# RWKV chunk maps taken off the state chain, early transfers placed elsewhere, and output transposes for two chunks

## The chip, the cores and the metric

One NeuronCore of a Trainium2 chip runs the whole program. Its engines are TensorE (PE, with its weight loads listed as PEld), VectorE (DVE), ScalarE (ACT), GpSimd (POOL) and SyncE (SP, which here only issues transfers); 16 DMA engines move data. The metric is the device time of one execution in microseconds, the median of several runs. PE's granted clock is given as a share of its full 2.4 GHz; 0.5 is its other level, 1.2 GHz.

## The reference

One layer of an encoder is computed for 1024 prompt rows and 64 sample rows of width 1024. All branches take columns of one projection.

```python
u = rms_norm(h);  z = u @ w_in
A: RWKV-7 (8 heads of 64): per step
   sa = S @ -kk;  S = S*w + sa*(kk*a) + v*k;  y = S @ r      # S: 64 x 64 state
   y = group_norm(y)*lnx_w + lnx_b + (sum(r*k*r_k))*v
B: forgetting attention, softmax(q.k/8 + c[t] - c[s]), causal
C: indexer scores -> top 256 keys -> grouped-query attention + T5 bias
h = h + concat(A*silu(gA), B*silu(gB), C*silu(gC)) @ w_out;  out = rms_norm(h)
```

The new states (RWKV state, keys, values, log forget gates, index keys) are outputs too.

## The kernel before

**Stages.** (1) Rows are loaded, normed and transposed; the indexer projects its keys and queries, and `weave` alternates its scoring with "fill". (2) RWKV: 17 units of four 64-step chunks (a unit is one pair of heads and four chunks; the last unit is the sample, one chunk for each pair). (3) Forgetting attention ("fox"). (4) Sparse attention ("dsa") and the output product.

**Fill** is the projection of all other columns, written as generators whose every step is one eighth of a projection: three matmuls at L154. `pump(rate)` adds to a credit after each step of a main generator and takes fill steps for it; `need(name)` drains fill up to a name. Fill is PE's work for moments in which the stage itself has none.

**RWKV.** In iteration u `braid` interleaves the steps of `tail` (unit u-2), `chain` (u-1), `chunk_invert` and `value_rows` (u) and `prepare` (u+1) by evenly spread positions, and the top-k search beside them; every step pumps R_A/10 = 0.7 fill steps. `chunk_invert` inverts a 64x64 triangular matrix per chunk and head by five doubling levels in float16 and gives `UD`. `chain` carries the state S: for each chunk a product of S with `QR` (`pa`, L1545), VectorE's `za` (L1546), a product with `UD` (`pb`, L1550), two VectorE copies to `UV` (L1555), products with `BA` into the state (L1558) and VectorE's new S (L1563), then the outputs from `BA` and `QR` (L1567, L1569). All five products work on 64x64 or 128x64 pieces of PE's array, one for each head; a float32 product is two instructions. `tail` norms the outputs, transposes one chunk at a time (four transposes of 128x64) and applies scale and bias on ScalarE (L1617).

**First transfers.** The index keys `KI` and `KIL` are computed on partitions 0 to 63 and copied to 64 to 127 by two transfers from GpSimd's queue (L443, L444). `relative_bias` multiplies a small table and stores it 128 times over (L1244, 1536 KB) to DRAM for the dsa stage. SP issues nearly all other transfers, in one order. The index keys' output is stored at L457, L458. `rwkv_pools` opens RWKV's buffers, loads `wabr` and splits it (L1262, L1264).

The instructions are put in order at build time by a list scheduler: an instruction that is written later can be placed earlier on its engine if its inputs are ready there.

Of the kernel before, what the change touches and what calls it, by code (L numbers as in the profile page):

```python
# [12 lines left out]
F32 = mybir.dt.float32  # L13
# [11 lines left out]
P = 128  # L25
# [60 lines left out]
class K:  # L86
# [149 lines left out]
    def braid(self, work, rate, side=None):  # L236


        order = sorted(((k + 0.5) / n * (0.4 if work[j][0] == "rows" else 1), j) for j, (_, _, n) in enumerate(work) for k in range(n))
# [30 lines left out]
    def setup(self):  # L270
# [12 lines left out]
        self.lnx = cp.tile([64, 16], F32, name="lnx")  # L283
# [4 lines left out]
        with ExitStack() as c2:  # L288
# [17 lines left out]
            lrows = xb[:16, 2 * P:2 * P + 64]  # L306
            nc.sync.dma_start(out=lrows[0:8, :], in_=I["a_lnx_w"].rearrange("x (a p) -> (x a) p", p=64))
            nc.sync.dma_start(out=lrows[8:16, :], in_=I["a_lnx_b"].rearrange("x (a p) -> (x a) p", p=64))
            ps = self.pt.tile([P, 4, P], F32, tag="xps", name="ps_setup").rearrange("p a b -> p (a b)")
            nc.tensor.transpose(ps[:, :46], rows[:46, :], self.ident[:46, :46])  # L310
            nc.tensor.transpose(ps[:64, 64:80], lrows, self.ident[:16, :16])
            nc.vector.tensor_copy(self.par[:, :46], ps[:, :46])
            nc.vector.tensor_scalar(self.lnx, ps[:64, 64:80], 0.5, None, op0=OP.mult)
# [84 lines left out]
    def indexer(self):  # L398
# [6 lines left out]
        with ExitStack() as c2:  # L405
# [10 lines left out]

            def keys(t0, n):
                ps = yield from self.proj(wm, t0, n)
                nc.scalar.copy(mT[:76, t0:t0 + n], ps[:76, :n])
                self.split2(ps[0:64, :n], None, KI[0:64, t0:t0 + n], KIL[0:64, t0:t0 + n])  # L420
# [19 lines left out]
            nc.scalar.copy(KI[0:64, 1088:1600], ps[:64, :])  # L440
            nc.vector.tensor_tensor(KIL[0:64, 1088:1600], ps[:64, :], KI[0:64, 1088:1600], op=OP.subtract)
# [15 lines left out]
            nc.sync.dma_start(out=O["p_c_kidx"][0, 0].rearrange("(a p) d -> p a d", p=P), in_=mrow[:, 0:8, 0:64])  # L457
            nc.sync.dma_start(out=O["s_c_kidx"][0, 0], in_=mrow[:64, 8, 0:64])  # L458
            for i in list(range(2, 8)) + ["s"]:
                if i == 4:  # L460
                    self.forget(ip, mrow)
                if i == 5:
                    self.relative_bias()
# [22 lines left out]
    def forget(self, ip, mrow):  # L486
# [26 lines left out]
        v.scalar_tensor_tensor(x, a, -2.0, x, op0=OP.mult, op1=OP.add)  # L513
        nc.sync.dma_start(out=O["p_b_logf"][0, 0].rearrange("(a p) h -> p a h", p=P), in_=x[:, 0:8, :])
# [714 lines left out]
    def relative_bias(self):  # L1229

        nc = self.nc
        self.d_t5 = self.dram.tile([P, 8, 384], F32, tag="d_t5", name="d_t5")
        with ExitStack() as c2:
            p = self.pool("t5", ctx=c2, right=True)
            pp = self.pool("t5p", space=PSUM, ctx=c2, right=True)
            tb = p.tile([32, 8], F32, name="t5tab")
            oh = p.tile([32, 384], F32, name="t5oh")
            nc.sync.dma_start(out=tb, in_=self.I["t5_table"])
            nc.sync.dma_start(out=oh, in_=self.I["onehot"])
            ps = pp.tile([P, 512], F32, name="t5ps")  # L1240
            nc.tensor.matmul(ps[:8, :384], tb, oh, start=True, stop=True)
            vv = p.tile([8, 384], F32, name="t5v")
            nc.vector.tensor_copy(vv, ps[:8, :384])
            nc.sync.dma_start(out=self.d_t5.rearrange("q h r -> h q r"), in_=vv.rearrange("h (o r) -> h o r", o=1).broadcast_to([8, P, 384]))  # L1244


    def rwkv_pools(self, c2):
# [20 lines left out]
        for t in self.ND:  # L1268
            nc.gpsimd.memset(t, 0.0)
# [12 lines left out]
    def elem(self, one, slots, x):  # L1282
# [13 lines left out]
        zt = one.tile([P, 2, N], F32, tag="zt", name="zt", bufs=2)  # L1296
        QR = one.tile([P, 4, 3, 64], F32, tag="QR", name="QR", bufs=3)
# [75 lines left out]
    def chunk_rows(self, one, x):  # L1373
# [9 lines left out]
        BA = one.tile([P, 2, 4, 128], F32, tag="BA", name="BA", bufs=3)  # L1383
# [29 lines left out]
    def value_rows(self, one, x, sample):  # L1413
# [13 lines left out]
        P1 = one.tile([P, 4, 64], F32, tag="P1", name="P1", bufs=2)  # L1427
        UV = one.tile([P, 2, 4, 64], F32, tag="UV", name="UV", bufs=2)
        lo, hi = slice(0, 64), slice(64, 128)
        x.update(P1=P1, UV=UV)  # L1430
# [5 lines left out]
        sc.copy(UV[lo, 1], q2[hi, :, 1])  # L1436
        yield
# [6 lines left out]
        sc.copy(P1, ps[:, :256].rearrange("p (c t) -> p c t", t=64))  # L1444
# [33 lines left out]
    def chunk_invert(self, one, x):  # L1478
# [37 lines left out]
        UD = one.tile([P, 4, 64], F32, tag="UD", name="UD", bufs=2)  # L1516
        v.scalar_tensor_tensor(UD, U, -1.0, each(at(R), at(U)), op0=OP.mult, op1=OP.subtract)
        x.update(UD=UD)
        yield

    def chain(self, one, slots, x):
# [3 lines left out]
        G = self.gring("gc", 1)  # L1525
        hv = (slice(0, 64), slice(64, 128))
        i64 = self.con[:, C_I64:C_I64 + 64]
        QR, UD, P1, BA, UV, Pt = x["QR"], x["UD"], x["P1"], x["BA"], x["UV"], x["Pt"]
        sample = slots[0][1] == 16
        s0 = x.get("s0")  # L1530
        if sample:
            send = one.tile([P, 256], F32, tag="e1", name="s_end").rearrange("p (c t) -> p c t", t=64)
        Yt = one.tile([P, 4, 64], F32, tag="Yt", name="Yt", bufs=2)
        ends = []
        ch, ab = G(), self.gring("gd", 1)()
        for c, (hp, t) in enumerate(slots):
            S = s0[:, hp] if sample else self.state
            if t == 0:
                S = one.tile([P, 64], F32, tag="S", name="S", bufs=2)
                v.memset(S, 0.0)  # L1540

            za, sp = [one.tile([P, 64], F32, tag=n, name=n) for n in ("za", "sp")]
# [43 lines left out]
    def tail(self, one, x):  # L1586
# [23 lines left out]
        for c in range(4):  # L1610
            self.turn(ps[0:64, c * P:c * P + P], Yt[:, c])
# [288 lines left out]
```

## Time and profile before

| what | value |
|---|---|
| median of 3 runs | 1339.45 us (1335.56 to 1340.52) |
| the profiled execution | 1332.74 us, span 1331.0 us |
| PE busy | 1264.6 us (95%) |
| DVE / ACT / POOL busy | 847.0 / 776.7 / 667.7 us |
| mean granted PE clock | 0.979 |

In the view of instructions in order of time, the first column is the start, the second how long it lasted; matmuls overlap in PE's pipeline, so what one costs is read from its start to the start of the next one, not from its duration. In the view by stretches, each engine's busy time stands with the count of instructions in brackets, then the granted clock, the share of the DMA engines and GB/s.

### The profile page before, as it was taken

The numbers are of one execution on the slowest core, as the hardware profiler recorded it, in microseconds if no ns is written. First come the engines' busy times: TensorE is split into PE (matmuls) and PEld (weight loads), VectorE is DVE, ScalarE is ACT, GpSimd is POOL, SyncE is SP. The second block draws the span as 40 slices with busy tenths as digits, with TensorE's granted clock in tenths as the row PEclk, the third lists the DMA queues.
The fourth block names the chain that finished last, engine by engine and source line by source line (L and its number), as shares of the span: only waits on it lengthen the run. The fifth ranks groups of instructions, "written<-read, shape, count | busy, mean of one in ns | idle before, by whom it ended". The sixth has DMA issues, their size and how long they took to land.

```text
span 1331.0 us, 29369 instructions
## 1 busy us (share of the span) xinstructions
PE 1264.6 (95%) x10563; PEld 963.3 (72%) x10563; DVE 847.0 (64%) x2483; ACT 776.7 (58%) x1758; POOL 667.7 (50%) x975
## 2 busy tenths in 40 slices
PE   7789999999999999988999998999999979999997
PEld 5567676777777777766777677888888856777764
DVE  7349437887777677889754316566666479666642
ACT  6235437777877878734353346677665568555532
POOL 6224454454445546555464365566667465444411
PEclk9999999999999999988999998999999989999999
DMA  7352423223223323433333378767755576543323
GB/s 224 71 109 67 133 82 98 62 62 94 63 70 110 95 80 127 136 94 111 101 104 112 117 215 250 219 193 216 189 171 157 145 206 182 145 116 108 92 75 96
DMA packets 172621, 169.60 MB, mean 127 GB/s; under 512 B 38546, under 2 KB 147130, under 8 KB 172475
## 3 DMA queue, kind: packets, MB, share of 16 engines
q1 hardware_dynamic: 172314, 166.89, 43.8%
q8 instruction: 84, 1.38, 0.4%
q0 software_dynamic: 160, 0.82, 0.3%
q14 instruction: 63, 0.51, 0.1%
HBM read 104.61 MB, written 62.24 MB: 125 GB/s over the span
## 4 chain that ended last, share of the span: by engine, by line
PE 75%; DVE 9%; DMA 8%; ACT 4%; issue 2%; SPq 1%; POOL 1%; DVEq 0%; POOLq 0%; ACTq 0%
PE pproj L154 33%; PE pproj L1683 7%; PE ps_pv L980 5%; PE ps_atp L107 5%; PE ps_tp L1683 4%; PE ps_ga L1398 3%; PE ps_sc L949 2%; DMA wraw<-in_w_in_dram 2%; PE ps_sc L950 2%; PE ps_gb L1457 2%; PE ps_gb L1464 1%; PE ps_tp L107 1%; ACT junka L588 1%; PE ps_gc L1567 1%; PE ps_gc L1558 1%
## 5 line engine op out<-in xcount | busy, mean ns | idle before, releaser
L154 PE MATMUL pproj<-uH,wh 128*128 128x384 f32 (+4 forms) x1088 | 493.7, 454 | 0.0
L154 PE MATMUL pproj<-uH,wl 128*128 128x384 f32 (+4 forms) x1088 | 363.3, 334 | 0.0
L154 PE MATMUL pproj<-uL,wb 128*128 128x384 bf16 (+4 forms) x1088 | 358.7, 330 | 0.4 <-DVE zg L770 0.4
L154 PEld LDWEIGHTS pproj<-uH,wh 128*128 128x128 f32 (+1 forms) x1088 | 217.2, 200 | 3.5 <-issue 0.4
L154 PEld LDWEIGHTS pproj<-uH,wl 128*128 128x128 f32 (+1 forms) x1088 | 207.7, 191 | 2.2 <-issue 0.2
L154 PEld LDWEIGHTS <-wb 128*128 128x128 bf16 (+1 forms) x1088 | 106.3, 98 | 116.6 <-issue 79.7
L588 ACT ACTIVATE junka<-score,tk_tau 128x1024 f16<-128x1024 f32 (+4 forms) x160 | 149.3, 933 | 44.0 <-DVE tk_tau L602 26.5
L901 POOL TENSOR_SCALAR S<-S,mx 128x128 f32<-128x128 f32 (+8 forms) x136 | 105.3, 777 | 85.9 <-DVE mx L900 64.6
L140 POOL TENSOR_TENSOR wl<-wraw,wh 128x256 fp32r<-128x256 f32 (+1 forms) x184 | 138.4, 782 | 6.1 <-ACT wh L137 3.8
L919 DVE TENSOR_TENSOR hl<-ps_atp,hl 128x512 fp32r<-128x512 f32 (+3 forms) x184 | 109.1, 600 | 50.1 <-ACT hl L918 49.0
L896 ACT ACTIVATE S<-S,mx 128x128 f32<-128x128 f32 (+8 forms) x136 | 105.7, 778 | 47.0 <-DVE mx L892 42.3
L918 ACT CAST hl<-ps_atp 128x512 fp32r<-128x512 f32 (+3 forms) x184 | 93.0, 514 | 64.9 <-PE ps_atp L107 56.0
L142 POOL TENSOR_SCALAR wb<-wraw 128x512 bf16<-128x512 f32 (+1 forms) x92 | 62.5, 696 | 119.7 <-issue 50.2
L980 PE MATMUL ps_pv<-hl,VS 128*128 128x256 f32 (+3 forms) x640 | 113.1, 290 | 6.7 <-ACT hl L918 3.2
L107 PE MATMUL ps_atp<-ident,S 128*128 128x128 f32 x616 | 102.9, 278 | 1.0 <-DVE hl L919 0.9
L980 PEld LDWEIGHTS ps_pv<-hl,VS 128*128 128x128 f32 (+1 forms) x640 | 89.4, 175 | 19.6 <-ACT hl L918 4.5
L1146 POOL TENSOR_TENSOR cb<-nm,T 128x256 f32<-128x256 bf16 (+2 forms) x80 | 48.8, 616 | 63.3 <-DVE mx L892 46.9
L107 PEld LDWEIGHTS ps_atp<-ident,S 128*128 128x128 f32 x616 | 75.6, 143 | 6.0 <-POOL cb L1146 1.2
L1683 PE MATMUL pproj<-oh,gh 128*128 128x512 f32 x144 | 69.2, 501 | 0.7 <-ACT oh L1662 0.4
L137 ACT CAST wh<-wraw 128x1024 fp32r<-128x1024 f32 (+1 forms) x46 | 47.7, 1037 | 36.5 <-PE pproj L154 29.1
L790 DVE SCALAR_TENSOR_TENSOR zm<-pproj,omm,zs 128x384 f32<-128x384 f32 (+2 forms) x52 | 25.7, 494 | 45.9 <-ACT zs L789 42.6
L1683 PE MATMUL pproj<-ol,gb 128*128 128x512 bf16 (+1 forms) x144 | 52.9, 391 | 0.7 <-DVE ol L1663 0.7
(385 smaller groups left out, 2858.1 us busy)
## 6 DMA issues: line engine op xcount, KB each, us to landing
wraw<-in_w_in_dram SPq DMA_DIRECT2D x45, 512.0 KB
oraw<-in_w_out_dram SPq DMA_DIRECT2D x12, 512.0 KB
out_dram<-rows SPq DMA_DIRECT2D x10, 512.0 KB
x<-in_x_prompt_dram SPq DMA_DIRECT2D x8, 512.0 KB
wt<-a_wa SPq DMA_DIRECT2D x16, 256.0 KB
b_v<-vs SPq DMA_DIRECT2D x8, 512.0 KB
VS<-b_v SPq DMA_DIRECT2D x8, 512.0 KB
d_y<-y SPq DMA_DIRECT2D x64, 64.0 KB
```

The source lines that it names most:

```text
L107: self.nc.tensor.transpose(out, x, self.ident[:n, :n])
L140: nc.gpsimd.tensor_tensor(l[:, k:k + 2, :n], raw[:, k:k + 2, :n], h[:, k:k + 2, :n], op=OP.subtract)
L142: nc.gpsimd.tensor_scalar(b[:, k:k + 4, :n], raw[:, k:k + 4, :n], 1.0, 0.0, op0=OP.mult, op1=OP.add)
L154: self.nc.tensor.matmul(ps[:n, :nt], a[:, k, :n], b[:, k, t0:t0 + nt], start=(k == 0 and i == 0), stop=(k == KD - 1 and i == 2))
L588: nc.scalar.activation(junk[:, :sc.shape[1]], sc, AF.Sign, bias=tf[:, j:j + 1], accum_out=cnt[:, j:j + 1])
L896: nc.scalar.activation(S[:, :kn], S[:, :kn], AF.Exp, bias=mx[:, nm - 1:nm], scale=-1.0, accum_out=mx[:, 6:7])
L901: nc.gpsimd.tensor_scalar(S[:, :kn], S[:, :kn], mx[:, 7:8], 0.5, op0=OP.mult, op1=OP.mult)
L918: nc.scalar.copy(ph[:kr, a:b], ps[:kr, a:b])
L919: nc.vector.tensor_tensor(pl[:kr, a:b], ps[:kr, a:b], ph[:kr, a:b], op=OP.subtract)
L980: nc.tensor.matmul(pv[0:m, q0:256], VS[:, kb, 0:m], hl[:, x, o:o + w], start=kb == 0 and x == 0, stop=at[-1][0] == last and n == 3)
L1146: nc.gpsimd.tensor_tensor(o, x, y, op=OP.add)
L1683: nc.tensor.matmul(ps[hf][:n, :], parts[m // 4][q][:, m % 4, :n], self.wo[m][q // 2][:, hf * 512:hf * 512 + 512], start=m == 0 and q == 0, ...
```

## The change

The two products of a chunk's state with matrices that don't depend on the state are put together ahead: with W, the product of `UD` and the turned `QR`, the new state is M0 S + S0 and the output M1 S + Y0. `chunk_maps` (at the end of `chunk_invert`) works out M, S0 and Y0 for a unit; M holds both heads' 64x64 blocks in a 128x128 matrix with zeros beside them. `chain` is then two full-array products and one VectorE instruction for each chunk. Buffers lose a copy: `zt`, `UV` and `UD` have one in place of two, `QR` and `BA` two in place of three, and `P1` (two) becomes half of `QP` (one). The products `pa` and `pb`, `za`, `sp`, the two copies and the four output products of each chunk are gone. `tail` transposes two chunks at once, and its two ScalarE instructions of 64x256 (L1617) become four of 64x128. `KI` and `KIL` are written to both halves by ScalarE and VectorE; the T5 table's load is written at block 3 of the scoring loop, its product at 5 and its store at "s", the gates' stores at 7 and the index keys' output at 4; `rwkv_pools` is called before `need("a0")`; the fill rate R_A goes from 7 to 7.5, and `braid` spreads `chain` over 0.7 of an iteration.

```diff
-        order = sorted(((k + 0.5) / n * (0.4 if work[j][0] == "rows" else 1), j) ...
+        order = sorted(((k + 0.5) / n * dict(rows=0.4, chain=0.7).get(work[j][0], 1), j) ...
...
-            lrows = xb[:16, 2 * P:2 * P + 64]
+            lrows = xb[:16, 2 * P:3 * P]
+            for c in (slice(0, 64), slice(64, P)):
+                nc.sync.dma_start(out=lrows[0:8, c], ...a_lnx_w); nc.sync.dma_start(out=lrows[8:16, c], ...a_lnx_b)
...
+            def both(ps, t0, n):
+                c = slice(t0, t0 + n)
+                for r in (slice(0, 64), slice(64, 128)):
+                    nc.scalar.copy(KI[r, c], ps[0:64, :n])
+                    nc.vector.tensor_tensor(KIL[r, c], ps[0:64, :n], KI[0:64, c], op=OP.subtract)
...
-            nc.gpsimd.dma_start(out=KI[64:128, :], in_=KI[0:64, :])
-            nc.gpsimd.dma_start(out=KIL[64:128, :], in_=KIL[0:64, :])
...
-            nc.sync.dma_start(out=O["p_c_kidx"]...)
-            nc.sync.dma_start(out=O["s_c_kidx"]...)
             for i in list(range(2, 8)) + ["s"]:
+                if i == 3:
+                    gates = self.forget(ip, mrow); next(gates)
+                    bias = self.relative_bias(c2); next(bias)
                 if i == 4:
-                    self.forget(ip, mrow)
+                    nc.sync.dma_start(out=O["p_c_kidx"]...); nc.sync.dma_start(out=O["s_c_kidx"]...)
                 if i == 5:
-                    self.relative_bias()
+                    next(bias)
+                if i == 7:
+                    next(gates, None)
+                if i == "s":
+                    next(bias, None)
...
-        for t in self.ND:
+        self.M = one.tile([P, 2, 4, 2, 64], F32, name="M")
+        for t in self.ND + [self.M]:
             nc.gpsimd.memset(t, 0.0)
...
+        sc.copy(QP[lo, :, 0], q2[lo, :, 0])
+        sc.copy(QP[hi, :, 0], q2[lo, :, 1])
...
+    def chunk_maps(self, one, x, UD):
+        for c in range(4):
+            for h in range(2):
+                nc.tensor.matmul(ps[hv[h], c * P:c * P + P], UD[hv[h], c], QP[hv[h], c] ..., start=True, stop=True)
+        sc.copy(W, q[:, :, 0])
+        for h in range(2):
+            sc.copy(UV[hv[h], h], q[hv[h], :, 1])
+        yield
+        for a in range(2):
+            for c in range(4):
+                for h in range(2):
+                    e = h if a == 0 else 1 - h
+                    nc.tensor.matmul(ch[hv[e], 256 * a + c * 64:...], BA[:, h, c, 64 * e:64 * e + 64], UV[:, h, c], ...)
+        v.tensor_tensor(S0, r3(ch[:, 0:256]), x["Pt"][:, :, 64:65].broadcast_to([P, 4, 64]), op=OP.mult)
+        sc.copy(Y0, r3(ch[:, 256:512]))
+        yield
+        for c in range(4):
+            for h in range(2):
+                nc.tensor.matmul(ps[hv[h], c * P:c * P + P], W[hv[h], c], BA[hv[h], h, c], start=True, stop=True)
+        for h in range(2):
+            v.tensor_tensor(M[hv[h], 0, :, h], q[hv[h], :, h], i64[hv[h]], op=OP.add)
+            v.tensor_tensor(M[hv[h], 1, :, 1 - h], q[hv[h], :, 1 - h], QR[hv[h], :, 0], op=OP.add)
+        yield
...
-            for h in range(2):
-                nc.tensor.matmul(pa[hv[h]], QR[hv[h], c, 1], S[hv[h]], start=True, stop=True)
-            v.tensor_tensor(za, pa, P1[:, c], op=OP.add)
-            sc.activation(sp, S, AF.Copy, scale=Pt[:, c, 64:65])
...
+            nc.tensor.matmul(ch[:, c * 64:c * 64 + 64], flat(M[:, 0, c]), S, start=True, stop=True)
+            nc.tensor.matmul(ch[:, 256 + c * 64:320 + c * 64], flat(M[:, 1, c]), S, start=True, stop=True)
+            v.scalar_tensor_tensor(self.state, ch[:, c * 64:c * 64 + 64], Pt[:, c, 64:65], S0[:, c], op0=OP.mult, op1=OP.add)
+            yield
-        sc.copy(Yt, ch[:, 256:512]...)
+        v.tensor_tensor(Yt, ch[:, 256:512]..., Y0, op=OP.add)
+        yield
...
-        for c in range(4):
-            self.turn(ps[0:64, c * P:c * P + P], Yt[:, c])
+        for j in range(2):
+            self.turn(ps[:, j * P:j * P + P], Yt[:, 2 * j:2 * j + 2].rearrange("p c t -> p (c t)"))
...
+        s.rwkv_pools(c2)
         s.need("a0")
...
-        s.rwkv_pools(c2)
...
-                work.append(("invert", s.chunk_invert(s.one, x[u]), 14, ()))
+                work.append(("invert", s.chunk_invert(s.one, x[u]), 17, ()))
...
-NCH=12
+NCH=6
...
-R_IDX, R_A, R_FOX, R_DSA1, N_TOPK,LATE = (70,5.5),7,1.56,2.32,17,1000
+R_IDX, R_A, R_FOX, R_DSA1, N_TOPK,LATE = (70,5.5),7.5,1.56,2.32,17,1000
```

## Rows read from the trace of the kernel before

**Rows 1.** Busy time by stretches; columns as told under the table of times.
```profile
55.00:95.00 40.00, 29.44 (x150) 21.30 (x150) 11.45 (x29) 12.14 (x25) 12.88 (x19) 0.87 0.52 95
95.00:200.00 105.00, 103.47 (x639) 76.71 (x637) 62.30 (x148) 47.12 (x96) 49.01 (x64) 1.00 0.33 98
200.00:762.00 562.00, 542.29 (x6196) 406.86 (x6195) 411.40 (x1266) 361.02 (x840) 286.10 (x436) 0.98 0.31 95
1062.00:1095.00 33.00, 25.00 (x123) 17.56 (x121) 26.65 (x93) 25.37 (x61) 21.06 (x33) 0.84 0.73 204
```

**Rows 2.** Who PE waited for from 200 to 762: total us, times, longest.
```profile
PE ps_gb L1457 <- DVE Y L1495: 2.6, 3, 1.6
```

**Rows 3.** PE in order of time, from 500.1: start, lasted, line, operands.
```profile
500.19 0.34 PE L1558 MATMUL ps_gc<-UV,BA 128*64 128x64 f32 x4
500.45 0.31 PE L1471 MATMUL ps_gb<-identh,U 64*64 64x64 f16 x8
...
501.20 0.27 PE L1569 MATMUL ps_gc<-S,QR 64*64 64x64 f32 x2
...
501.48 0.34 PE L154 MATMUL pproj<-uL,wb 128*128 128x384 bf16 x1
...
501.83 0.34 PE L154 MATMUL pproj<-uH,wl 128*128 128x384 f32 x1
502.01 0.34 PE L154 MATMUL pproj<-uL,wb 128*128 128x384 bf16 x1
```

**Rows 4.** The same view from 506.9.
```profile
506.94 0.34 PE L154 MATMUL pproj<-uH,wl 128*128 128x384 f32 x1
507.21 0.33 PE L1550 MATMUL ps_gd<-za,UD 64*64 64x64 f32 x4
507.47 0.34 PE L154 MATMUL pproj<-uL,wb 128*128 128x384 bf16 x1
```

**Rows 5.** The same view from 255.0.
```profile
255.04 0.68 PE L1443 MATMUL ps_ga<-UV,BN 64*64 64x64 f32 x16
255.65 0.29 PE L1464 MATMUL ps_gb<-T,ND 128*128 128x64 f16 x4
```

**Rows 6.** The same view from 509.1.
```profile
509.17 0.66 PE L1349 MATMUL ps_ga<-ident,arn 128*64 128x128 f32 x8
509.76 0.34 PE L154 MATMUL pproj<-uL,wb 128*128 128x384 bf16 x1
```

**Rows 7.** The same view from 857.3.
```profile
857.35 1.01 PE L1017 MATMUL ps_pv<-hl,VS 128*128 128x128 f32 x8
858.19 0.30 PE L107 MATMUL ps_atp<-ident,S 128*128 128x128 f32 x1
```

**Rows 8.** Single lines: count, duration ns min/median/max, first and last start, forms.
```profile
L1546 DVE TENSOR_TENSOR za<-ps_gd,P x68: 154/218/225, 205.9 to 755.1; 128x64 f32<-128x64 f32 x68
L1555 DVE COPY UV<-ps_gd x136: 192/222/230, 222.6 to 758.8; 64x64 f32<-64x64 f32 x136
L1402 DVE TENSOR_TENSOR BA<-ps_ga,con x34: 404/415/416, 183.8 to 703.2; 128x256 f32<-128x256 f32 x34
L1547 ACT ACTIVATE sp<-S,Pt x64: 331/347/357, 168.7 to 728.7; 128x64 f32<-128x64 f32 x64
L1617 ACT ACTIVATE yT<-ps_tp,lnx x40: 398/558/563, 258.0 to 777.8; 64x256 f32<-64x256 f32 x32, 64x64 f32<-64x64 f32 x8
```

**Rows 9.** Who PE waited for from 0 to 200: total us, times, longest.
```profile
PE ps_idx L472 <- DMA KI<-KI: 6.8, 1, 6.8
PE ps_idx L472 <- ACT rl L475: 3.7, 1, 3.7
```

**Rows 10.** SP's issues in order of time, 48 to 80: start, how long issuing took.
```profile
48.19 0.29 SPq L1244 DMA_DIRECT2D d_t<-t5v  x1
56.51 21.34 SPq L130 DMA_DIRECT2D wraw<-in_w_in_dram  x2
```

**Rows 11.** The chain of waits that ended last: start, us, what.
```profile
56.51 30.01 DMA wraw<-in_w_in_dram
```

More of the change, by code (lines that the diff above doesn't have):

```diff
@@ L236, in braid @@
     def braid(self, work, rate, side=None):
-        order = sorted(((k + 0.5) / n * (0.4 if work[j][0] == "rows" else 1), j) for j, (_, _, n) in enumerate(work) for k in range(n))
+        order = sorted(((k + 0.5) / n * dict(rows=0.4, chain=0.7).get(work[j][0], 1), j) for j, (_, _, n) in enumerate(work) for k in range(n))
         live = [True] * len(work)
@@ L1227, in dsa, with relative_bias @@
         return units()
-    def relative_bias(self):
+    def relative_bias(self, ctx):
         nc = self.nc
         self.d_t5 = self.dram.tile([P, 8, 384], F32, tag="d_t5", name="d_t5")
[L1233 to L1244, printed above, removed]
+        p = self.pool("t5", ctx=ctx, right=True)
+        pp = self.pool("t5p", space=PSUM, ctx=ctx, right=True)
+        tb = p.tile([32, 8], F32, name="t5tab")
+        oh = p.tile([32, 384], F32, name="t5oh")
+        nc.sync.dma_start(out=tb, in_=self.I["t5_table"])
+        nc.sync.dma_start(out=oh, in_=self.I["onehot"])
+        yield
+        ps = pp.tile([P, 512], F32, name="t5ps")
+        nc.tensor.matmul(ps[:8, :384], tb, oh, start=True, stop=True)
+        vv = p.tile([8, 384], F32, name="t5v")
+        nc.vector.tensor_copy(vv, ps[:8, :384])
+        yield
+        nc.sync.dma_start(out=self.d_t5.rearrange("q h r -> h q r"), in_=vv.rearrange("h (o r) -> h o r", o=1).broadcast_to([8, P, 384]))
     def rwkv_pools(self, c2):
@@ L1295, in elem @@
         wt = one.tile([P, 2, N], F32R, tag="wt", name="wt", bufs=2)
-        zt = one.tile([P, 2, N], F32, tag="zt", name="zt", bufs=2)
-        QR = one.tile([P, 4, 3, 64], F32, tag="QR", name="QR", bufs=3)
+        zt = one.tile([P, 2, N], F32, tag="zt", name="zt")
+        QR = one.tile([P, 4, 3, 64], F32, tag="QR", name="QR", bufs=2)
         BK = one.tile([P, 4, 3, 64], F32, tag="BK", name="BK")
@@ L1379, in chunk_rows @@
         dg = self.dg
-        BA = one.tile([P, 2, 4, 128], F32, tag="BA", name="BA", bufs=3)
+        BA = one.tile([P, 2, 4, 128], F32, tag="BA", name="BA", bufs=2)
         BN = one.tile([P, 2, 4, 64], F32, tag="BN", name="BN", bufs=NBN)
@@ L1572, in chain @@
             yield
-        sc.copy(Yt, ch[:, 256:512].rearrange("p (c t) -> p c t", t=64))
+        v.tensor_tensor(Yt, ch[:, 256:512].rearrange("p (c t) -> p c t", t=64), Y0, op=OP.add)
+        yield
         if ends:
@@ L1576, in chain @@
             n = len(ends)
-            so = one.tile([64, n, P], F32, tag="QR" if sample else "so", name="so", bufs=3 if sample else 1)
+            so = one.tile([64, n, P], F32, tag="QR" if sample else "so", name="so", bufs=2 if sample else 1)
             for i, (hp, s2) in enumerate(ends):
```

101 lines of the change are left out of this document (52 added, 49 removed).

## The prediction

> **What bounds it now.** I read the busy time by stretches first. From 200 to 762, RWKV with its fill, PE is busy 542.3 of 562 us; VectorE 411 and ScalarE 361 [rows 1]. So PE bounds the stage, and what counts is how long PE is held, not how long the chain of states takes: the list of who PE waited for has nothing in that stage above the 2.6 us for VectorE's `Y` [rows 2]. Two other stretches have holes. From 55 to 95 PE is busy 29.4 of 40 us at a granted clock of 0.87; from 1062 to 1095, where fill has run out, 25.0 of 33 at 0.84 [rows 1]. The first hole is two waits, 6.8 us for the `KI` copy and 3.7 for a ScalarE that stood before it [rows 9].
>
> **How PE time is read.** A busy PE is not the price of a product; the distance from one start to the next is. Between two full-array projections it is 0.18 us (501.83 to 502.01 [rows 3]); into a 64x64 product 0.27 [rows 4]. A change of the array's tile thus holds PE 0.09 us longer on the way in. Four float32 instructions of 64x64 (two side by side, two passes) hold it 0.26 up to the next full product [rows 4]; sixteen, that is eight passes, 0.61 [rows 5]. A further pass of 64 columns therefore costs (0.61 - 0.26)/6 = 0.058 us, and a lone visit of two passes 0.26 + 0.09. Four passes of 128 columns hold 0.59 [rows 6], and with 128x128 float32 weights a pass of 128 columns 0.84/8 = 0.105 [rows 7].
>
> **Chain and maps, on PE.** Before, a chunk has the product with `UD` (0.26 [rows 4]), two with `BA` (0.26 each, one of them from 500.19 to 500.45 [rows 3]) and the pair of `QR` products (0.28 501.20 to 501.48 [rows 3]): 1.06, with three entries at 0.09 1.33 us; 68 chunks (the count of `za` [rows 8]) give 90 us. After, a chunk is two full-array products, four passes of 64 columns. The trace has no such product. Its ends are 0.058 (64 columns, smaller tiles) and 0.105 (128x128 weights, 128 columns): 15.9 or 28.6 us for 68 chunks. I take 0.058, because the moving columns are the same; nothing less is to be had, since that row holds no switch. The maps cost, for each unit, two groups of eight passes of 128 columns (0.59 + 4 x 0.105 = 1.01 each; 1.18 if they are two visits), sixteen passes of 64 (0.26 + 14 x 0.058 = 1.07; at 0.105 1.68) and three entries, 0.27: 3.36 to 4.31, for 17 units 57 to 73 us. So 90 becomes 73 (value) or up to 102: -17, at worst +12.
>
> The Trainium skill ("TensorE: Matmul & The Clock Gate", section on LDWEIGHTS) says that a weight load takes the number of its columns divided by 1.2 GHz, whatever the rows; that is 107 ns for 128 columns, so by the page the chain's passes would cost the upper end and the sum would be -4 instead of -17. No row here shows a full-array float32 product with 64 columns.
>
> **Output transposes.** 68 become 34, each 128 columns at 0.105 [rows 7]: -3.6 us, and about one entry less per unit, 1.5: -5. ScalarE gets four half-size instructions for two of 0.56 us [rows 8]; by the 0.4 us of the smaller form in that row, +0.5 us a unit.
>
> **The other engines.** VectorE loses four `za` (0.22) and eight copies (0.22) [rows 8], 2.6 us a unit; S0, the sum into `Yt` and four instructions for M come, at most 0.42 each by the `BA` row [rows 8], 2.5. Even. ScalarE loses four `sp` (0.35 [rows 8]) and the copy to `Yt`, and gets six copies at about the same price: with the transposes +1 us a unit, 17 of a stage in which it is busy 361 of 562 us [rows 1]. Its cover is PE's work; without it the 17 us would show. The wait for M lies in `chain` at the front of PE's queue, behind three new steps PE-ScalarE-PE-VectorE-PE-VectorE that come after the inversion; queued behind it are the other generators' products and fill. So of PE's 22 us I count two thirds, -15.
>
> **Fill.** Steps for each iteration were 3 + 13 + 15 + 3 + 9 = 43 (each generator's yields and its last call), at 0.7; now 3 + 6 + 18 + 3 + 9 = 39 at 0.75: 30.1 becomes 29.3 fill steps. The last chain, pumped at 2.66, has 7 steps fewer: -19; the first preparation +4. Together 28 steps leave RWKV. One step holds PE 0.53 us (501.48 to 502.01 [rows 3]), so 15 us go to later stages. That is no gain by itself, but the hole at 1062 begins where fill ends, with 8 us idle and 33 x 0.16 = 5 us of clock [rows 1]. I take -4; bounds 0 and -13.
>
> **First stage.** The two `KI` copies leave GpSimd's queue; the wait of 6.8 us goes. What is late next: the projection weights that SP issued at 56.5 (issuing alone took 21.3 for two [rows 10]) landed 30.0 us later [rows 11], at 86.5, and the second wait is theirs, by way of ScalarE, which casts them. Before them in SP's order stands the 1536 KB table store of 48.2 [rows 10]. The change writes it at a later line, but the list scheduler places a transfer where its input is ready, as it already did here (written after the scoring of two blocks, issued before any); so I expect it at 48 again, and the weights still decide when PE goes on. I take -3, the share of the queue that the copies gave back; bounds -10.5 (both waits) and +5 if the store lands on a later weight. The eight added ScalarE and VectorE instructions lie in a stretch where those engines are 12 of 40 us busy [rows 1]; cost 0, at most 3 without that. The moved gate, index-key and `wabr` transfers pass SP's queue in another order; the whole idle time of PE from 95 to 200 is 1.5 us [rows 1], so 0 (-1 to +1); so for the two more setup transfers.
>
> **The sum.** -15 - 4 - 3 = -22. From the profiled execution's 1332.7 that is 1311. The median of the runs shown is 6.7 higher, 1339.45; for it, **1317.5 us**.
>
> **Rivals.** (a) *The weights of a full-array product bind* (0.105 a pass): chain 28.6, PE -9, two thirds -6, with -4 and -3: -13, 1326. For it: the only row with 128x128 weights and few columns [rows 7]; against: that row moves 128 columns, which may be its whole price. The Trainium skill's LDWEIGHTS rule is this case.
>
> (b) *Nothing is left*: maps and chain both at the upper prices, +12, transposes -5, fill and first stage -7: 1339. It needs every unknown at its worst.
>
> (c) *Slower: the path through a unit sets the pace.* Inversion and maps are now 18 dependent steps in one iteration, in place of 15, and M, S0, UV and QP have one copy, so that a unit's maps can't begin before the chain before has read them. If that path is longer than a unit's PE work, a unit (562/17 = 33 us [rows 1]) doesn't get shorter: the -15 is gone, 15 us of fill still move later and cost 11 net, first stage -3: +8. With 0.3 us of each new step uncovered, 15 more: +23 at most, +13 taken, 1352. It decides when 18 steps take over 31 us, 1.7 each. For it: VectorE and ScalarE carry the search beside it. Against: PE waited only 2.6 us for `Y`, on the ten level steps of 17 units [rows 2].
>
> (d) *All of it*: PE's 22 whole, the hole closed, both first waits gone (-10.5): -43, 1297.
>
> **How the numbers follow.** Forecast 0.50, (a) 0.16, (b) 0.13, (c) 0.13, (d) 0.08. The predicted time is the forecast's, 1317.5. The range goes from just inside (d) to past (b), 1299 to 1345, and leaves out (c) and the far part of (d). A measurement of this kernel can tell about 0.5% from no change, 1333 to 1346: faster 0.71 (forecast, a, d, less a little), same 0.15, slower 0.14.
>
> **What would show it.** Right: in the RWKV stretch PE's starts at `chain` are 0.25 us a chunk apart from the next work, no tile change around them; `chunk_maps` holds PE 3.4 us a unit; the stage ends 25 to 35 us earlier; fill ends near 1062 or later with the hole smaller. Table store near 48 us again and weights 25 us or more under way. Wrong: a PE waiting for M, W or `Y` over 15 us in total (c), chain passes 0.1 us apart (a), or the first hole gone or moved behind 95 us.

## The result, and the profile after

The changed kernel takes 1387.59 us (median; 1384.09 to 1392.63) beside 1337.51 for the kernel before on the same chip: a ratio of 1.0397, 95% interval 1.0369 to 1.0426. It is 50 us slower; 1317.5 was predicted. Its profiled execution took 1392.63 us, span 1390.8 us, 60 us more than the one before, at a mean granted clock of 0.964 in place of 0.979.

Busy time by stretches of the changed kernel, to be laid beside [rows 1]; RWKV now ends near 812, and the last line is the stretch in which fill runs out.

```profile
55.00:95.00 40.00, 27.08 (x144) 19.73 (x143) 10.75 (x27) 10.24 (x22) 12.79 (x19) 0.83 0.51 91
95.00:200.00 105.00, 102.31 (x606) 76.08 (x604) 60.83 (x139) 45.38 (x89) 42.43 (x58) 0.97 0.31 92
200.00:812.00 612.00, 558.25 (x6183) 441.03 (x6182) 408.91 (x1177) 387.14 (x897) 286.89 (x440) 0.96 0.29 88
1062.00:1095.00 33.00, 31.93 (x214) 25.55 (x212) 15.83 (x60) 15.11 (x47) 19.11 (x39) 1.00 0.69 190
1135.00:1165.00 30.00, 25.16 (x117) 16.21 (x117) 22.48 (x61) 20.90 (x45) 13.81 (x20) 0.83 0.78 230
```

Before, PE idled 20 of 562 us of RWKV; now 54 of 612. VectorE's work is no more than it was (409 for 411 us), ScalarE's grew by 26. The hole where fill ends has moved from 1062 to 1135. In its own stretch PE idles 4.8 us where it idled 8.0, but behind the last `UD` it idles 32.5 us in all, and 25.3 before:

```profile
783.40:1390.80 607.40, 574.93 (x3548) 452.92 (x3567) 338.79 (x981) 338.98 (x766) 305.76 (x442) 0.98 0.57 162
```

Before:

```profile
735.80:1331.00 595.20, 569.87 (x3537) 444.15 (x3537) 336.08 (x986) 335.26 (x758) 304.72 (x435) 0.98 0.57 160
```

**A unit.** To compare kernels I take the stretch from the start of VectorE's `UD` of unit 1 to that of unit 14, thirteen units; the lines begin and end some 0.3 us ahead of these starts. Before:

```profile
248.20:681.50 433.30, 416.47 (x4768) 313.12 (x4762) 336.48 (x1026) 294.28 (x683) 229.48 (x347) 0.97 0.32 97
```

After:

```profile
264.40:726.50 462.10, 419.05 (x4693) 330.75 (x4689) 326.30 (x936) 302.12 (x699) 216.48 (x329) 0.96 0.28 87
```

Divided by 13: a unit went from 33.33 to 35.55 us, PE's busy time from 32.04 to 32.23, PE's idle time from 1.29 to 3.31. PE was to lose 1.3 us of work a unit and about one fill step; it lost nothing, and it waits 2 us more.

**Where the profiled 60 us lie.** `UD` of the first unit starts at 229.2 (220.4 before), that of the last at 783.4 (735.8), and the span ends at 1390.8 (1331.0): 9 us ahead of RWKV's first `UD`, 39 in the 16 units, 12 behind.

**The clock.** With two levels, a mean of 0.979 over the span is some 56 us at 1.2 GHz, and 0.964 some 100 us. One such stretch, and the one ahead of it, in which PE was busy 5.2 of 6.8 us:

```profile
636.00:642.80 6.80, 5.20 (x46) 4.03 (x46) 6.47 (x13) 3.29 (x8) 6.72 (x8) 1.00 0.61 205
642.80:656.50 13.70, 11.25 (x66) 8.49 (x65) 11.20 (x26) 3.31 (x8) 7.89 (x9) 0.50 0.19 65
```

A step of fill takes 0.96 us there, and 0.53 at the full clock [rows 3]:

```profile
650.76 0.51 PE L154 MATMUL pproj<-uL,wb 128*128 128x384 bf16 x1
651.72 0.49 PE L154 MATMUL pproj<-uL,wb 128*128 128x320 bf16 x1
```

So 0.45 of the time at the lower level is lost. For the 44 us more, that is an estimate of at most 20 of the profiled 60 us; in the thirteen units, where it is 24 and 33 us, some 4 of the 29. Whether PE's added waits brought the clock down, no run separates.

**Who PE waited for**, 200 to 812 (total us, times, longest), for [rows 2]:

```profile
PE ps_gb L1483 <- ACT T L1528: 9.3, 7, 3.2
PE ps_gb L1576 <- ACT W L1553: 5.9, 9, 1.1
PE ps_gb L1476 <- DVE Y L1514: 4.9, 10, 1.1
...
PE ps_gb L1476 <- DVE Y L1532: 2.5, 4, 1.4
...
PE ps_gb L1483 <- DVE T L1519: 1.9, 5, 0.4
...
PE ps_gd L1604 <- DVE M L1581: 0.8, 1, 0.8
```

**One passage from unit to unit**, PE in order of time (start, lasted, operands; where an engine idled before, that stands at the end):

```profile
369.32 0.42 PE L1476 MATMUL ps_gb<-U,Y 64*64 64x64 f16 x8
...
370.66 1.09 PE L1550 MATMUL ps_gb<-QP,UD 64*64 64x128 f32 x16
...
372.23 1.09 PE L1576 MATMUL ps_gb<-BA,W 64*64 64x128 f32 x16
...
375.37 1.15 PE L1564 MATMUL ps_gc<-UV,BA 128*64 128x64 f32 x30
376.45 0.31 PE L1490 MATMUL ps_gb<-identh,U 64*64 64x64 f16 x8
```

The same on VectorE:

```profile
366.71 0.49 DVE L1508 TENSOR_TENSOR U<-U,con 128x256 f16<-128x256 f16 x1
...
369.79 0.42 DVE L1536 SCALAR_TENSOR_TENSOR UD<-U,ps_gb 128x256 f32<-128x256 f16 x1 [0.95 <-PE ps_gb L1476]
...
373.37 0.42 DVE L1581 TENSOR_TENSOR M<-ps_gb,con 64x256 f32<-64x256 f32 x1 [2.46 <-PE ps_gb L1576]
```

And on ScalarE:

```profile
371.80 0.37 ACT L1553 COPY W<-ps_gb 128x256 f32<-128x256 f32 x1 [1.50 <-PE ps_gb L1550]
...
376.74 0.37 ACT L1452 COPY UV<-ps_ga 64x256 f32<-64x256 f32 x1
...
378.27 0.37 ACT L1510 COPY T<-ps_gb 128x256 f16<-128x256 f16 x1
```

The next unit's `U` was ready at 367.2. Its first products (L1490) come at 376.45, behind the maps of the unit that ended with `UD` at 369.79; `T`, which on ScalarE stands behind four copies of `value_rows` (two of them new, to `QP`), starts 8.5 us after `UD`. The same passage before the change, on VectorE and ScalarE:

```profile
344.45 0.42 DVE L1517 SCALAR_TENSOR_TENSOR UD<-U,ps_gb 128x256 f32<-128x256 f16 x1
344.87 0.35 ACT L1491 COPY T<-ps_gb 128x256 f16<-128x256 f16 x1
```

Over the first 15 units `T` starts 8.2 us after the last `UD` on average, before the change 0.9 (-0.6 to 2.7); from `T` to `UD` it is 27.4 us, before 31.6. The two together are always the unit, so they don't say what bounds it; they say that the change put 7.3 us between `UD` and `T` and took only 4.2 out of the inversion beside the other work.

**The short chain on PE**, for [rows 3] and [rows 4]:

```profile
238.32 0.33 PE L154 MATMUL pproj<-uH,wl 128*128 128x384 f32 x1
238.50 0.33 PE L1604 MATMUL ps_gd<-ST,M 128*128 128x64 f32 x2
238.66 0.39 PE L1605 MATMUL ps_gd<-ST,M 128*128 128x64 f32 x2
238.98 0.66 PE L1366 MATMUL ps_ga<-ident,arn 128*64 128x128 f32 x8
```

A chunk holds PE 0.16 + 0.32 = 0.48 us here. In 58 of the 68 chunks the four instructions stand together with no idle time behind them; there the median is 0.48 too (0.36 to 0.68).

**The first stage**: who PE waited for from 0 to 200, for [rows 9], and SP's issue of the table store, for [rows 10]:

```profile
PE ps_tp L454 <- ACT mrow L455: 10.9, 1, 10.9
```

```profile
48.64 0.29 SPq L1259 DMA_DIRECT2D d_t<-t5v  x1
56.83 17.87 SPq L130 DMA_DIRECT2D wraw<-in_w_in_dram  x2
```

The copy to `mrow` that PE waits for stands on ScalarE behind a cast of projection weights:

```profile
84.46 1.04 ACT L137 CAST wh<-wraw 128x1024 fp32r<-128x1024 f32 x1 [16.47 <-DMA wraw<-in_w_in_dram]
...
85.78 0.21 ACT L455 COPY mrow<-ps_tp 128x76 f32<-128x76 f32 x1
```

### The profile page after: what moved, and what is told of

It reads as the page before. It is cut to its first block, busy times and chain, and to the rows that moved or that the text cites. A ratio compares the mean times of both kernels' runs of the same rounds, so it can differ in the third digit from the quotient of the medians.

```text
span 1390.8 us, 29233 instructions
## 1 busy us (share of the span) xinstructions
PE 1282.6 (92%) x10510; PEld 1003.5 (72%) x10529; DVE 845.5 (61%) x2385; ACT 803.4 (58%) x1811; POOL 658.8 (47%) x974
## 5 line engine op out<-in xcount | busy, mean ns | idle before, releaser
L154 PE MATMUL pproj<-uH,wh 128*128 128x384 f32 (+4 forms) x1088 | 504.7, 464 | 0.0
L154 PE MATMUL pproj<-uH,wl 128*128 128x384 f32 (+4 forms) x1088 | 367.8, 338 | 0.0
L154 PE MATMUL pproj<-uL,wb 128*128 128x384 bf16 (+4 forms) x1088 | 364.1, 335 | 3.8 <-DVE shift L807 2.0
L154 PEld LDWEIGHTS pproj<-uH,wh 128*128 128x128 f32 (+1 forms) x1088 | 221.6, 204 | 6.2 <-issue 2.6
L154 PEld LDWEIGHTS pproj<-uH,wl 128*128 128x128 f32 (+1 forms) x1088 | 212.3, 195 | 2.2 <-issue 0.2
L915 POOL TENSOR_SCALAR S<-S,mx 128x128 f32<-128x128 f32 (+8 forms) x136 | 101.8, 752 | 84.7 <-DVE mx L914 59.7
L140 POOL TENSOR_TENSOR wl<-wraw,wh 128x256 fp32r<-128x256 f32 (+1 forms) x184 | 134.4, 761 | 7.4 <-ACT wh L137 5.0
L142 POOL TENSOR_SCALAR wb<-wraw 128x512 bf16<-128x512 f32 (+1 forms) x92 | 59.7, 666 | 164.7 <-PE pproj L154 80.4
L1725 PE MATMUL pproj<-ol,gb 128*128 128x512 bf16 (+1 forms) x132 | 49.8, 397 | 1.1 <-DVE ol L1705 0.7
```

Of the source, the lines that this page charges most:

```text
L140: nc.gpsimd.tensor_tensor(l[:, k:k + 2, :n], raw[:, k:k + 2, :n], h[:, k:k + 2, :n], op=OP.subtract)
L142: nc.gpsimd.tensor_scalar(b[:, k:k + 4, :n], raw[:, k:k + 4, :n], 1.0, 0.0, op0=OP.mult, op1=OP.add)
L154: self.nc.tensor.matmul(ps[:n, :nt], a[:, k, :n], b[:, k, t0:t0 + nt], start=(k == 0 and i == 0), stop=(k == KD - 1 and i == 2))
L915: nc.gpsimd.tensor_scalar(S[:, :kn], S[:, :kn], mx[:, 7:8], 0.5, op0=OP.mult, op1=OP.mult)
L1725: nc.tensor.matmul(ps[hf][:n, :], parts[m // 4][q][:, m % 4, :n], self.wo[m][q // 2][:, hf * 512:hf * 512 + 512], start=m == 0 and q == 0, ...
```

## The experiments

All ratios are to the kernel before on the same chip, with 95% intervals; the times of a unit are read as above.

### Which part of the change costs the 50 us

Each run holds a part of the change's own diff and nothing else: all of it but the first-stage, `lnx` and output-transpose hunks; the first-stage hunks with the earlier `rwkv_pools`; the output-transpose hunks; and the last two together.

> The kernel before with the maps part alone: chunk_maps, the short chain, the cut buffers, the fill rate 7.5 and the spread of 0.7; first transfers and output transposes as before. Theory P (the maps stand in a row with the inversions: their three steps lie between one unit's UD and the next unit's first T, so a unit takes longer although PE has less to do): this part carries the loss, +35 to +50 us, a unit near 34.6 us from UD to UD, and 5 us or more from UD to the next T. Rival F (the moved first transfers carry it): this part alone is within 10 us of the kernel before, or faster by the 15 us that were predicted.

Measured: 1.0375 (1.0331 to 1.0420), 1386.24 us. A unit 35.81 us, `T` 7.9 us behind `UD`. The maps part alone is the whole loss; the cut buffers, the fill rate and the spread of `chain` are in it.

> The kernel before with the first-stage part alone: KI written twice, the loads, gates, index-key and table transfers at their new places, the pools of RWKV opened earlier. Theory P: +5 to +10 us (the first UD came 9 us later in the changed kernel, with a wait of 10.9 us for mrow), all of it before the first UD. Rival F: +25 us or more, with RWKV's units longer than before too. The prediction's step: -3.

Measured: 0.9972 (0.9945 to 1.0000). The first `UD` at 224.3, 4 us later than before, and the total still no longer: neither theory's loss is there, the prediction's -3 is within the interval.

> The kernel before with output transposes for two chunks at once alone. Prediction's step: -5 us of PE, of which two thirds realised, so -3 (at 1.5 us less entry cost) and not slower. Rival: ScalarE's four instructions in place of two hold up T and the other copies that PE waits for: +3 or more, with a longer unit.

Measured: 0.9985 (0.9954 to 1.0017). The prediction's -3 us is within it, and so is nothing.

> The kernel before with the first-stage part and the two-chunk output transposes together, without the maps part. Alone they measured 0.9972 and 0.9985 of the kernel before. If they add up: 0.9957, 5 to 6 us faster, 1328 beside 1334. Rival: the first-stage part's gain is lost in the second state of the sequence (it starts RWKV 4 us later), and the two together are within 0.2% of no change.

Measured: 1.0022 (1.0008 to 1.0036). They don't add up to a gain. Without the maps, what is left of the change is no faster than the kernel before.

### Place, buffers and fill

```diff
-        D = self.gring("gb", 2)
+        D = self.gring("gc", 1)
```

> The changed kernel with one line other: the products for W and for M go to the PSUM buffer gc in place of the two buffers gb that they share with the inversion. Theory P1 (the shared buffers tie the next unit's first products to the maps' reads): the time from UD to the next unit's T falls from 6-11 us to under 5 and 10 us or more come back. Theory P2 (the order of the program, not the buffers, puts the inversion behind the maps): within 5 us of the changed kernel. Theory P3 (W, S0/Y0 and M now in one buffer are more in a row than before): slower by 5 or more.

Measured: 1.0491 (1.0445 to 1.0537). P1 was right on what holds `T` back, it now starts 1.4 us after `UD`, and P3 on the price: from `T` to `UD` it takes 34.2 us in place of 27.4, and a unit 36.44.

Next, the maps out of the inversion:

```diff
-        yield from self.chunk_maps(one, x, UD)
+        x.update(UD=UD)
...
     def chain(self, one, slots, x):
+        yield from self.chunk_maps(one, x)
...
-        D = self.gring("gb", 2)
+        D = self.gring("gc", 1)
...
-dict(rows=0.4, chain=0.7)
+dict(rows=0.6, chain=0.7)
...
-NCH=6
+NCH=9
```

The inversion counts 14 steps again in place of 17.

> The changed kernel with chunk_maps taken out of the inversion and put ahead of the chain in the next iteration, so that the next unit's inversion is written beside it and not behind it; its products use gc, and value_rows stands a little later (0.6 for 0.4). All arithmetic stays. Theory P2 (the written order puts the inversions behind the maps, and that is what a unit's 2.4 us come from): the next T again 0 to 3 us after UD, a unit back to 32 us, RWKV 25 to 40 us shorter than in the changed kernel, so 1345 to 1360. Rival L (PE's waits come from VectorE and ScalarE having too much to do in a unit, wherever the maps stand): within 8 us of the changed kernel.

Measured: 1.0378 (1.0347 to 1.0410), 1383.61 us. `T` starts 1.3 us after `UD`, as P2 wanted, but the inversion beside it takes 32.4 us. A unit:

```profile
257.50:705.00 447.50, 413.10 (x4688) 326.22 (x4690) 331.57 (x940) 308.88 (x712) 223.78 (x336) 0.98 0.29 90
```

34.42 us, PE busy 31.78. The place is worth 1.1 of the 2.2 us in these profiles, half of which goes with a granted clock of 0.98 for 0.96, and nothing that the total could tell (1.0378 for 1.0397). P2 as the whole cause falls.

> As the run with the maps in the next iteration, and QR with three buffers, as before the change, in place of two. Theory B (the buffers that the change took hold up the input transfers and with them the units): another 5 us or more faster than with two. Theory P2: the same within 4 us, because the inputs of a unit were there in time.

Measured: 1.0367 (1.0327 to 1.0407), 1383.29 us. A third `QR` changes nothing.

```diff
-R_IDX, R_A, ... = (70,5.5),7.5,...
+R_IDX, R_A, ... = (70,5.5),9,...
```

> The changed kernel with the fill rate at 9 in place of 7.5 (35 steps of fill for a unit in place of 29). Theory I (PE idles in RWKV behind the inversions, and fill would use it): the units stay near 34.6 us, some 85 steps of fill go back into RWKV, what follows RWKV is 15 to 40 us shorter. Rival Q (fill steps hold their place in PE's queue, so more of them only make a unit longer): the units grow by most of the 3 us that six steps take, and the time stays within 10 us of the changed kernel.

Measured: 1.0552 (1.0509 to 1.0595). Rival Q holds for the units: they grew to 38.01 us, 2.5 for six steps. The total did not stay within its 10 us, it is some 20 us above the changed kernel. The part behind the last `UD` got 16 us shorter for 100 fill steps less, at a granted clock of 0.94 there in place of 0.98. PE's idle time of 3.3 us a unit can't be had by more fill: it fell to 2.6. A lower rate in the changed kernel was not run.

The kernel before with R_A = 5.8 for 7:

> The kernel before with the fill rate at 5.8 in place of 7 (25 steps of fill for a unit in place of 30), nothing else. Theory PE (PE bounds RWKV in the kernel before, as the prediction took it): RWKV gets 35 to 45 us shorter, the fill that it loses comes later at the same price: the total within 15 us of the kernel before. Theory S (the row of inversions already sets the pace before the change, and fill only fills it): a unit keeps its 32 us, and the total grows by 25 to 45 us.

Measured: 1.0210 (1.0177 to 1.0242).

```profile
246.80:655.80 409.00, 379.41 (x4536) 285.74 (x4538) 327.94 (x1033) 283.60 (x658) 201.43 (x308) 0.97 0.27 82
```

PE's busy time fell by 2.85 us a unit (32.04 to 29.19), the unit by 1.87 (33.33 to 31.46), PE's idle time rose from 1.29 to 2.28; `T` to `UD` takes 30.3 us and the next `T` follows after 0.6. So less work on PE does shorten a unit, but not by all of it: something else begins to hold it near 31 us. Both theories are half right: RWKV got 24 us shorter from the first `UD` to the last (35 to 45 by Theory PE), and the total grew by 28 us, as Theory S has it. Behind the last `UD` 98 more fill steps took 55 us more, 0.56 each.

### The price of each piece, taken out and put back

The kernels of this part leave work out, as their expectations say.

```diff
-        yield from self.chunk_maps(one, x, UD)
+        x.update(S0=self.Z[0], Y0=self.Z[1])
+        yield
+        yield
+        yield
```

> The changed kernel without chunk_maps: its products, copies and sums are left out, M, S0 and Y0 stand at zero, the three steps stay empty so that fill is taken as before; the short chain works on the zeros. In the changed kernel a unit takes 35.5 us from UD to UD (the mean of units 2 to 14). Theory W (PE's own work for the maps, 3.4 us a unit, is the price, two thirds of it realised): a unit falls by 2 to 2.5 us. Theory P (the row inversion-maps is the price): by 4 to 6, with the next T at UD again.

Measured: 0.9819 (0.9797 to 0.9841).

```profile
259.70:659.40 399.70, 363.72 (x3860) 285.72 (x3860) 294.63 (x862) 287.92 (x659) 215.94 (x331) 0.99 0.32 99
```

A unit falls by 4.8 us to 30.75, with PE idle 2.77 of it: Theory P's number.

```diff
-            nc.tensor.matmul(ch[...], flat(M[:, 0, c]), S, ...); nc.tensor.matmul(ch[...], flat(M[:, 1, c]), S, ...)
-            v.scalar_tensor_tensor(self.state, ...)
+            self.state = S0[:, c]
```

> As the kernel without maps, and without the chain's products and state sums as well; the Yt sum is taken from zeros. It is RWKV without any state path. Against it the short chain's price is read (kernel without maps minus this): 0.7 us a unit by the prediction's 0.058 a pass, 1.1 by 0.105 a pass, each with two thirds realised, over 2 if VectorE's four round trips count. And the old chain's price (before, 33.3 us a unit, minus this): 3.5 us by the prediction's 1.33 us a chunk with two thirds realised; under 2.5 means that there was less to be had than predicted.

Measured: 0.9737 (0.9713 to 0.9761). The short chain costs 0.0082, 11 us; a unit without any state path is no shorter than with the short chain (30.98 us, at a granted clock of 0.94 in place of 0.99):

```profile
257.70:660.50 402.80, 356.28 (x3712) 274.64 (x3707) 303.33 (x822) 289.75 (x663) 226.49 (x337) 0.94 0.33 100
```

The third run keeps the maps' matmuls and takes out every instruction that reads their PSUM, with constant tiles for W, UV, S0 and Y0:

> The changed kernel with the 40 products of chunk_maps left on PE at their places, but nothing taken out of PSUM: W, UV, S0, Y0 and M are constant zeros, so no copies or sums on ScalarE and VectorE and no round trips. Theory W: a unit stays within 0.7 us of the changed kernel's 35.5. Theory P (round trips and evictions are the price): 2 us or more shorter than that, near the kernel without maps.

Measured: 1.0225 (1.0199 to 1.0250).

```profile
269.70:714.70 445.00, 418.17 (x4661) 330.43 (x4661) 300.18 (x859) 284.99 (x645) 212.50 (x330) 0.98 0.29 89
```

A unit is 34.23 us, 1.3 shorter than the changed kernel's and so between the two theories; PE's busy time is 4.2 above that without maps (32.17 for 27.98). The products alone are 0.0406 of the time, 54 us; what they hand to the other engines adds 0.0172, 23 us.

The same three deletions in the kernel with the maps at the head of the chain:

> The maps' products alone (on constant zeros, nothing taken out of PSUM), as in the earlier run with products alone, but written at the head of the next iteration's chain, beside the next inversion and not ahead of it. That run took 1.0225 of the kernel before, the kernel without maps 0.9819. Theory W (PE's time is the price): 1.015 to 1.03 again. Theory P (the place ahead of the next inversion is the price): 0.985 to 1.005.

Measured: 1.0138 (1.0105 to 1.0170). A little under Theory W's range, well over P's: off the row the products cost 0.032 in place of 0.041.

```diff
-        for c in range(4):
-            for h in range(2):
-                nc.tensor.matmul(ps[hv[h], c * P:c * P + P], UD[hv[h], c], QP[hv[h], c]...)
+        nc.tensor.matmul(ps[:, 0:64], flat(UD[:, 0:2]), QP[:, 0, 0], start=True, stop=True)
```

The same is done to the other two groups, and the copies and sums read these 64 columns four times.

> The changed kernel with one full-array product of 64 columns in place of each of the maps' three groups (three products instead of 40); all copies and sums of the maps stay, and each waits for its product (M is made zero by a product with zeros). So the round trips and ScalarE's and VectorE's work are there, PE's work nearly not. The kernel without maps took 0.9819. Theory W: 0.985 to 0.995, the round trips hide behind fill as those of the inversion do. Theory P: 1.005 or more, because three steps more lie in a row.

Measured: 1.0039 (1.0011 to 1.0067).

```profile
257.40:678.90 421.50, 378.97 (x3939) 297.72 (x3935) 322.03 (x934) 301.02 (x699) 217.21 (x328) 0.99 0.31 94
```

Nearly Theory P's number: with hardly any of the maps' work on PE (29.15 us busy a unit), a unit is 1.7 us longer than without maps, and PE idles 3.27 us; `T` comes 6.2 us after `UD` in place of 1.4. The profiled execution is the fastest of ten, 8 us under their median. The copies, the sums and their round trips cost 0.022, 29 us, with hardly any products.

The kernel before without its chain, and with the chain's matmuls alone (their moving operands constant zeros):

> The kernel before without its chain: the products, za, sp, the copies to UV and the state sums are left out, outputs and states are zeros, the steps stay for fill. If the changed kernel without any state path (0.9737) is the same program but for buffers and small moves: 0.970 to 0.978, and the old chain cost 22 to 30 of 1000. If the cut buffers cost something there: under 0.965.

Measured: 0.9695 (0.9663 to 0.9727).

```profile
252.40:658.40 406.00, 362.12 (x3748) 277.24 (x3748) 300.54 (x806) 275.70 (x624) 220.31 (x343) 0.95 0.33 101
```

The whole old chain cost 0.0305, 41 us, a little over the 22 to 30 of 1000. Without it PE is busy 4.2 us a unit less, but the unit is 2.1 us shorter (31.23), and PE idles 3.4.

> The kernel before with the old chain's products alone: all 20 instructions of a chunk at their places with their weights, but the moving data are constant zeros, nothing is taken out of PSUM ahead of the outputs, and no product waits for another chunk. Theory W (the chain cost what it held PE): 0.99 to 1.00, nearly the whole of the old chain. Theory L (its round trips made its price, its products lay in PE's gaps): under 0.985.

Measured: 1.0148 (1.0114 to 1.0181): slower than with the whole chain, which neither theory allowed. Freed of their waits, the products are put elsewhere by the scheduler: in the thirteen units PE turns to the chain 8.2 times a unit in place of 13.4. What VectorE waited for in this run, 258.6 to 710.1 (total us, times, longest):

```profile
DVE Y L1497 <- PE ps_gb L1466: 37.6, 29, 3.7
DVE T L1502 <- PE ps_gb L1459: 21.4, 26, 2.6
```

The same two in the kernel before, 248.2 to 681.5:

```profile
DVE Y L1495 <- PE ps_gb L1464: 6.5, 15, 0.9
DVE T L1500 <- PE ps_gb L1457: 5.4, 8, 2.1
```

That the inversion's steps stood behind longer visits fits these waits; it is not shown as the cause of the longer time. The granted clock was lower too, 0.971 to 0.977 in this run's executions, with a mean of 0.980 before. That raised the question whether the maps cost so much because they come in lumps of 16 instructions:

```diff
                 nc.tensor.matmul(ps[hv[h], c * P:c * P + P], UD[hv[h], c], QP[hv[h], c]...)
+            if c < 3:
+                yield
```

So too in the other two groups; QP and UV get two buffers, and R_A / 10 becomes 0.61 for the added steps. `chain` is spread over 0.6 here and `rows` over 0.4, and the last chain's rate is 1.52 for 2.66: these too differ from the uncut kernel.

> The kernel with the maps at the head of the next iteration's chain (1.0378 of the kernel before), with each of the maps' three product groups cut into steps of one to two chunks (10 steps in place of 4 for the maps), so that fill and the inversion's products are written between the pieces; QP and UV have two buffers, the fill rate for a step goes down so that a unit gets the same 29 fill steps. No product is added or taken away. Theory K (it is the lumps: the inversions' steps decide the pace, and 16 instructions, 1.0 us, stand ahead of a ready step, as the clumped products of the old chain did): 1.02 to 1.03, VectorE's waits for PE at Y and T shorter. Theory W (PE's sum of work decides, however it is cut): 1.033 to 1.045.

Measured: 1.0415 (1.0366 to 1.0465). It doesn't decide: the scheduler put the pieces together again, PE turns to chain and maps 8.2 times a unit where the uncut kernel did 7.2 times. Whether small pieces would hide better is open.

## Why the prediction was wrong

The prices, as differences of the ratios above times 1335 us (each uncertain by some 5 us), beside the prediction's terms, its two thirds taken:

| term | predicted | measured | from |
|---|---|---|---|
| old chain gone | -60 (90 x 2/3) | -41 | 1 - 0.9695 |
| short chain | +11 (15.9 x 2/3) | +11 | 0.9819 - 0.9737 |
| maps' products | +38 (57 x 2/3) | +54 | 1.0225 - 0.9819 |
| maps' copies, sums, round trips | 0 | +23 | 1.0397 - 1.0225 |
| buffers and all the rest of the program without a state path | -10 (transposes, fill, first stage) | +6 | 0.9737 - 0.9695 |
| sum | -21 | +53 | |

The pieces are taken out in one order; another order would share the loss out otherwise (the copies and round trips with hardly any products came to 29 us, not 23). The clock is in the prices too. By the 0.45 found above, the lower level costs an estimated 24 us in the kernel before, 36 without the old chain, 41 without any state path, 30 without the maps, 28 with the maps' products alone and 41 in the changed kernel (mean granted clocks 0.980, 0.969, 0.965, 0.974, 0.978, 0.967). At one clock the old chain would be worth some 12 us more, the short chain cost 11 more and the maps' copies and sums 14 less. In every case the maps cost more than the old chain gave back.

**What bounds the kernel** was read too simply, and this is the step that failed: that PE's time alone sets the length of RWKV, so that two thirds of any PE time come back and PE's work covers what the other engines do. PE's 32.0 us a unit did bound it, but a second limit lay 1 us or so below. In four runs with less work on PE (27.4 to 29.2 us a unit) a unit stops at 30.75 to 31.46 us, and PE idles 2.3 to 3.6 us of it. The clock is not that limit: in the run without maps it is 0.99. The list of PE's waits [rows 2] couldn't show it, because the old chain's products and fill stood in PE's gaps: without the chain PE idles 2.1 us a unit more. What hints at it is that `T` starts 0.9 us after the last `UD`, a distance I didn't read. That the second limit is this row of inversions is argued, not shown: the way from `T` to `UD` has no fixed length (26.3 us in the run with short products, 34.2 with the other PSUM buffer), and no run took work off VectorE or ScalarE and left that row as it was. The share of PE time that is realised isn't two thirds for every piece.

**Old chain**: PE's time was about right (from start to start 84.2 us in all, 6 of them idle, 90 predicted; its 1.33 us a chunk are 1.05 by PE's busy time, 4.2 us a unit). But half of it lay in gaps: without it PE idles 2.1 us a unit more, and only 41 us come back.

**Maps on PE**: well sized, 57.1 us from start to start (20.3 for L1550, 19.4 for L1564, 17.4 for L1576) for 57. They were realised whole, 54 us, and not for two thirds. A part of that is their place between `UD` and the next `T`: at the head of the chain they cost 0.032, 43 us.

**Maps on the other engines**: "even" for VectorE and "+1 us a unit" for ScalarE was right as busy time (VectorE 25.9 to 25.1 us a unit, ScalarE 22.6 to 23.2) and wrong as a price. The prediction put this term at nothing and named PE's work as the cover, 17 us without it; 23 came. The instructions wait for one another in three round trips, and the run with short products has 29 us from them with hardly any of the maps' products on PE.

**Short chain**: 0.48 us a chunk in the row above, 31.6 us in all from start to start, not 0.25 and 15.9. The price on PE is that of rival (a). That the total came to the 11 us of the prediction is luck: twice the time on PE, a third of it realised. The lower clock of the run without it hides some of the price, and that the short chain is cheap because it stands beside the row is argued only. The Trainium skill ("TensorE: Matmul & The Clock Gate", section on LDWEIGHTS) gives 107 ns for a load of 128 columns; an estimate of four of them is 0.43 us. The trace agrees with that for the four passes together, 0.48, but not for each, since the first two took 0.16.

**Rival (c)** came closest: the path through a unit, with its condition (over 31 us; a unit is 35.5). Its sign fell just short: PE waited for M, W and `Y` 14.1 us in all where over 15 was the mark, and 11.2 for `T`, which was not named. It was priced at 1352, with PE's saving as lost; that PE's work doesn't fall and the products cost their whole time was not in it.

**Fill**: 28 steps were to leave RWKV; between the first `UD` and the last state they fell from 508 to 482. They were to find a hole and be worth -4. The hole went along with the end of fill, 1062 to 1135, and the part behind the last `UD` is 12.2 us longer. In the two runs with other rates a step that goes later costs 0.56 us, one that goes earlier brings 0.16, the latter with the lower clock told there.

**First stage**: the table store stands at 48.6 as foreseen, the `KI` wait is gone, and 10.9 us for `mrow` came in its place; PE idles 12.9 us from 55 to 95, and 10.6 before. That wait is the one for the weights, by way of ScalarE, as the prediction had it: issued at 56.8, they are cast at 84.5, 27.6 us later. Alone this part is 0.9972, within the bounds given.

**Open** is what the second limit is, and what stretches the inversion from 27 to 32 us when the maps stand beside it and not ahead of it (PE's sum of work, its lumps, or ScalarE and VectorE, which carry more copies at once), how far PE's waits bring the lower clock, and why the old chain's products alone cost more than the whole chain.

## What to carry to other kernels

An engine that hardly ever idles doesn't prove that it alone sets the pace: look for a row of dependent steps that follows itself without a gap from one unit to the next, and test it by taking work off the engine; here 4.2 us less work made a unit 2.1 us shorter. Work that is put between the end of one unit's row and the start of the next can cost its whole time and its round trips; elsewhere pieces cost a third to three quarters of what they held the engine (11 of 31.6, 41 of 84, 43 of 57). To price a change of algorithm in such a loop, take the old piece out and see what the loop is worth without it: here that was 41 us, so a replacement had to cost less than that, and its products alone took 54.

## What was not expected of the hardware

Two full-array float32 products of 64 columns (four passes) hold PE 0.48 us in the row shown, where sixteen instructions on 64x64 pieces of the array, eight passes, held it 0.61 [rows 5]: with full weights a pass of as many columns cost half as much again on average (0.12 for 0.076), and the second product twice the first (0.32 for 0.16). And the old chain's products without their waits, and without the VectorE and ScalarE instructions between them, made a longer program (1.0148 for 1.0). They were issued in fewer, longer visits; that this is the reason is not shown.
